# Who issues the four small copies ahead of each rotary multiply: SyncE or GpSimd

## The chip, the core and the metric

The kernel runs on one core of one Trainium2 chip. The metric is device microseconds of one execution; a measurement of this kernel can tell about 0.5% (6.4 us) from no change.

## What is computed

Two layers of a streaming encoder run on a prompt of 1024 tokens and a sample of 32 tokens with a past of 256, with shared weights. Layer 0 has a convolution branch and a forgetting attention. Layer 1 has a pooling branch and a sparse attention: a small indexer (4 heads of 64) scores all keys, each query keeps its best 256 (a threshold), and 8 heads of 64 attend under that mask. In layer 1 the queries, keys, index queries and index keys are rotated by their position:

```python
def rope(x, pos):
    ...
    x1, x2 = xf[..., : d // 2], xf[..., d // 2:]
    return jnp.concatenate([x1 * cos - x2 * sin, x2 * cos + x1 * sin], -1).astype(x.dtype)
```

## The kernel before, in words

Work is tiled with channels on the 128 partitions and up to 544 tokens along the row. A projection of 128 channels is 4 token groups of 24 matmuls (`proj_steps`, L207; operands are split in a high and a low part, so three products per block). While a projection runs on TensorE (PE), `tick` after every 8 matmuls runs deferred steps and background generators, so other stages are woven between.

A rotary call (`rope`, L982) works on a tile `rpx` [128, 544] that ScalarE (ACT) has filled from PSUM (L979, or L1209). Channel halves are 32 partitions apart, so `rope` first makes a copy `rps` with neighbouring blocks of 32 partitions exchanged: one DMA per block (L986), SBUF to SBUF, two for the 64 index-key channels and four for 128 channels. GpSimd (POOL) multiplies `rps` by the sine table (L987), VectorE (DVE) multiplies `rpx` by the cosine table in place (L988) and adds the two (L989). There is one buffer `rps`, so the copies of a call wait until the add of the call before has read it; L988 overwrites `rpx`, so it waits until the copies have landed.

There are 22 calls, 84 copies. In this text they are numbered in their order:

- ropes 0 and 1: index keys (64 channels, two copies each); ropes 2 to 5: index queries (two projections, each a 256-token and a 544-token half, four copies each). This is the index stage. Its results feed the index scores (L288, L289, then L1258 on ACT and L1260, L1262 on DVE), on which DVE's threshold search (L1088) and ACT's (L1112) stand.
- ropes 6 to 9: key and query of the first head pair (`qk1(0)`), while the masks are made (L1349 to L1391).
- ropes 10 to 21: key and query of the next three pairs, woven into the attention of the pair before (`attend`). After a key rope, `put_k` splits the result and `k_out` transposes it on PE (L295) for the output; after a query rope, `put_q` (L280 to L285) fills query tiles whose zero halves POOL writes (`blank_q`, L275 and L276).

All DMAs of the kernel before are issued by SyncE (SP), in one queue: weights (`wraw`, L114), value rows (`vf`, L448), gates (`sg`, L385), spills (L330, L331), outputs (`vo`, L1315; `ko`, L297) and the copies of L986. Every engine works through its own list in order; an instruction that waits holds up all behind it. The order of these lists is made by the scheduler of the tile framework from the program order, its priorities and its own cost model, so a change of who issues a DMA also moves other instructions.

Of the kernel before, what the change touches and what calls it, by code (L numbers as in the profile page):

```python
# [32 lines left out]
def tile_encoder(ctx: ExitStack, tc, A, O):  # L33
    nc = tc.nc
    pe, dve, act, pool, sp = nc.tensor, nc.vector, nc.scalar, nc.gpsimd, nc.sync
# [645 lines left out]
    with tc.tile_pool(name="p1", bufs=1, reuse_waits="tile") as p1:  # L681
# [82 lines left out]
        xs = p1.tile([128, 8, 128], FR, name="xs", tag="xrow", bufs=3)  # L764
# [217 lines left out]
    def rope(pl, x, t0, n, rows=128):  # L982
        xs = pl.tile([128, 544], FT, name="rps", tag="rps", bufs=1)
        for b in range(rows // 32):
            s = b ^ 1
            sp.dma_start(xs[32 * b:32 * b + 32, :n], x[32 * s:32 * s + 32, :n])  # L986
        pool.tensor_tensor(xs[:rows, :n], xs[:rows, :n], sinT[:rows, t0:t0 + n], op=OP.mult)  # L987
        dve.tensor_tensor(x[:rows, :n], x[:rows, :n], cosT[:rows, t0:t0 + n], op=OP.mult)  # L988
        dve.tensor_tensor(x[:rows, :n], x[:rows, :n], xs[:rows, :n], op=OP.add)  # L989
# [172 lines left out]
    with tc.tile_pool(name="p4", bufs=1, reuse_waits="tile") as p4:  # L1162
# [9 lines left out]
        def ev_ik(g, t0, n, ps):  # L1172
            act.activation(ikw[64:68, t0:t0 + n], ps[64:68], AF.Copy, scale=0.5)
            r = rope_in(p4, hold, "ik", g, ps[0:64], 1.0, 64)
            if g % 2 == 0:
                return
            t0, n = t0 - 256, n + 256
            rope(p4, r, t0, n, 64)
            cs = slice(t0, t0 + 512)
            act.activation(ikw[0:64, t0:t0 + n], r[0:64, :n], AF.Copy)  # L1180
            act.activation(kiA[0:64, cs], r[0:64, :512], AF.Copy)
            act.activation(kiB[64:128, cs], r[0:64, :512], AF.Copy)
            dve.tensor_tensor(kiA[64:128, cs], r[0:64, :512], kiA[0:64, cs].bitcast(FT), op=OP.subtract)
            dve.tensor_tensor(kiB[0:64, cs], r[0:64, :512], kiA[0:64, cs].bitcast(FT), op=OP.subtract)
# [16 lines left out]
        for p in range(2):  # L1201
            qA, qB = (p4.tile([128, SEQ - 256], FR, name=f"{nm}{p}") for nm in ("qiA", "qiB"))
            qz = blank_q(p4, f"qiz{p}", SEQ - 256)
            qi_st.append((qz, qA, qB))

            def ev_iq(g, t0, n, ps, p=p, qz=qz, qA=qA, qB=qB):
                if g == 1:
                    hold["iq"] = p4.tile([128, 544], FT, name="rpx", tag="rpx", bufs=2)
                    act.activation(hold["iq"][:, 256:512], ps, AF.Copy, scale=0.125)  # L1209
                    x, t0, n = hold["iq"][:, 256:512], 256, 256  # L1210
                else:
                    x = rope_in(p4, hold, "iq", g, ps, 0.125)
                    if g % 2 == 0:
                        return
                    t0, n = t0 - 256, n + 256
                rope(p4, x, t0, n)
                m = min(n, 512)
                cs = slice(t0 - 256, t0 - 256 + m)
                put_q(qz[:, :, cs], qA[:, cs], qB[:, cs], x[:, :m])
                if n > 512:  # L1220
                    dve.tensor_copy(iqS[:, p, :], x[:, 512:544])
            proj_cm(w1, 3072 + p * 128, 128, X1, ev_iq, range(1, 4))
# [265 lines left out]
    def qk1(p):  # L1488
# [6 lines left out]
        def ev_k(g, t0, n, ps):  # L1495
            r = rope_in(pq, hold, "k", g, ps, 1.0)
            if g % 2:
                rope(pq, r, t0 - 256, n + 256)
                put_k(kA, kB, t0 - 256, 512, r[:, :512])
                defer(6, k_out, 1, p, g // 2, n + 256, r, pq)  # L1500
                if n > 256:
                    dve.tensor_copy(qkS1[:, p, 1, :], r[:, 512:544])
# [106 lines left out]
```

## Time and profile before

| | us |
|---|---|
| median of 3 runs | 1274.49 |
| lowest and highest run | 1273.25, 1278.46 |
| the profiled execution's own time | 1278.22 |
| its span in the trace | 1276.2 |
| PE busy in the span | 1198.5 |
| DVE, ACT, POOL busy | 983.4, 712.5, 256.2 |
| granted TensorE clock, mean | 0.987 |

The profile page gives the busy time of each engine, the chain of work that ended last, and groups of instructions by line; the trace behind it can be asked for the instructions of a stretch in order of time, with the idle time before each and what ended it. Times in the trace are microseconds from the start of the span. Instructions that only issue a DMA are listed under their queue's engine (SPq for SP) and not counted as busy.

### The profile page before, as it was taken

To read this page: it belongs to the slowest core of one execution; us is meant where nothing else is said; L and a number is where in the kernel's file an instruction comes from. 1 tells how busy PE (TensorE), PEld (TensorE's weight loads), DVE (VectorE), ACT (ScalarE), POOL (GpSimd) and SP (SyncE) were. 2 spreads that over 40 slices of the span, in tenths; PEclk is the share of its full clock that TensorE was granted. 3 is DMA by queue.
4 is the path that set the end of the run, shared out by engine and by line. 5 is a ranking of instruction groups with operands and counts; after the bars stand their busy time and mean duration, and the time that the engine had idled before them with its cause. 6 is when DMAs were issued, how large, how long until landed. Compare 5 with 4: busy or idle time off the path is not lost.

```text
span 1276.2 us, 25219 instructions
## 1 busy us (share of the span) xinstructions
PE 1198.5 (94%) x9353; PEld 1136.2 (89%) x9353; DVE 983.4 (77%) x2053; ACT 712.5 (56%) x1533; POOL 256.2 (20%) x590
## 2 busy tenths in 40 slices
PE   8999999999998989999989979999898999879997
PEld 6999999988898977999988979999888888869997
DVE  5699999357877878558759958897678978886477
ACT  5111242378787876321366768888467778875110
POOL 0000033002433333000120336566211111100000
PEclk9999999999999999999999989999899999999999
DMA  7113422336322284642342232322323222633512
GB/s 223 51 34 97 122 54 63 94 100 187 85 84 84 67 260 131 192 131 101 112 106 62 69 84 68 84 64 64 85 68 97 71 72 80 199 117 123 161 38 99
DMA packets 163302, 130.29 MB, mean 102 GB/s; under 512 B 35850, under 2 KB 151010, under 8 KB 163180
## 3 DMA queue, kind: packets, MB, share of 16 engines
q1 hardware_dynamic: 163180, 128.69, 34.0%
q8 instruction: 73, 1.20, 0.4%
q14 instruction: 49, 0.40, 0.1%
HBM read 82.93 MB, written 40.31 MB: 97 GB/s over the span
## 4 chain that ended last, share of the span: by engine, by line
PE 59%; DVE 15%; ACT 14%; issue 5%; DMA 3%; SPq 1%; POOL 1%; DVEq 0%; ACTq 0%; POOLq 0%
PE bank L207 27%; PE bank L571 14%; PE bank L240 4%; PE bank L419 3%; ACT jka L1112 3%; PE bank L394 3%; DVE wt L1088 2%; ACT s L373 2%; PE bank L288 2%; ACT pth L107 2%; DVE ptl L108 1%; PE bank L289 1%; DVE s L370 1%; PE bank L223 1%; PE bank L252 1%
## 5 line engine op out<-in xcount | busy, mean ns | idle before, releaser
L870 DVE SCALAR_TENSOR_TENSOR acc<-apad,vT,acc 128x1086 f32<-128x1086 f32 x120 | 156.3, 1342 | 1.1
L108 DVE TENSOR_TENSOR ptl<-bank,pth 128x512 fp32r<-128x512 f32 (+1 forms) x160 | 99.1, 633 | 38.6 <-ACT pth L107 37.3
L207 PE MATMUL bank<-x1h,whi 128*128 128x256 f32 (+3 forms) x848 | 127.3, 289 | 0.1
L207 PE MATMUL bank<-x1h,wlo 128*128 128x256 f32 (+3 forms) x848 | 127.3, 291 | 0.0
L207 PE MATMUL bank<-x1l,whi 128*128 128x256 f32 (+3 forms) x848 | 126.3, 289 | 0.0
L207 PEld LDWEIGHTS bank<-x1h,wlo 128*128 128x128 f32 (+1 forms) x848 | 115.8, 193 | 1.6
L207 PEld LDWEIGHTS bank<-x1h,whi 128*128 128x128 f32 (+1 forms) x848 | 113.5, 189 | 1.9 <-ACT rpx L979 0.3
L207 PE MATMUL bank<-x0h,whi 128*128 128x256 f32 (+1 forms) x768 | 113.4, 288 | 1.5 <-ACT kr L810 1.0
L207 PEld LDWEIGHTS bank<-x1l,whi 128*128 128x128 f32 (+1 forms) x848 | 113.7, 190 | 0.9
L373 ACT ACTIVATE s<-s,mn 128x896 f32<-128x896 f32 (+7 forms) x128 | 98.8, 773 | 24.7 <-DVE mn L370 23.6
L419 PE MATMUL bank<-ident,s 128*128 128x128 f32 x576 | 96.2, 279 | 17.4 <-DVE ptl L108 10.8
L207 PE MATMUL bank<-x0h,wlo 128*128 128x256 f32 (+1 forms) x768 | 111.7, 286 | 0.0
L207 PE MATMUL bank<-x0l,whi 128*128 128x256 f32 (+1 forms) x768 | 110.4, 284 | 0.0
L108 DVE TENSOR_TENSOR wlo<-wraw,whi 128x1024 fp32r<-128x1024 f32 (+2 forms) x62 | 75.3, 1215 | 43.2 <-ACT whi L107 43.2
L107 ACT ACTIVATE pth<-bank 128x512 fp32r<-128x512 f32 (+1 forms) x160 | 85.8, 549 | 34.3 <-PE bank L419 32.3
L207 PEld LDWEIGHTS bank<-x0h,whi 128*128 128x128 f32 x768 | 101.2, 189 | 3.7 <-ACT kr L810 1.3
L207 PEld LDWEIGHTS bank<-x0h,wlo 128*128 128x128 f32 x768 | 100.8, 189 | 0.8
L207 PEld LDWEIGHTS bank<-x0l,whi 128*128 128x128 f32 x768 | 100.0, 188 | 0.7
L1112 ACT ACTIVATE jka<-sc,neg 128x768 bf16<-128x768 f32 (+2 forms) x96 | 99.3, 1035 | 2.0
L107 ACT ACTIVATE whi<-wraw 128x1024 fp32r<-128x1024 f32 (+2 forms) x62 | 65.0, 1050 | 55.7 <-PE bank L207 36.0
L394 PE MATMUL bank<-pth,v 128*128 128x256 f32 x320 | 92.0, 306 | 3.6 <-ACT pth L107 3.2
L419 PEld LDWEIGHTS bank<-ident,s 128*128 128x128 f32 x576 | 66.2, 140 | 32.6 <-DVE ptl L108 12.2
(422 smaller groups left out, 2695.0 us busy)
## 6 DMA issues: line engine op xcount, KB each, us to landing
wraw<-in_o_w_in_dram SPq DMA_DIRECT2D x26, 512.0 KB, 4.0
wraw<-in_e_w_in_dram SPq DMA_DIRECT2D x24, 512.0 KB, 4.1
sgd<-sgc SPq DMA_DIRECT2D x32, 128.0 KB, 3.0
out_dram<-ko SPq DMA_DIRECT2D x16, 256.0 KB, 2.3
vf<-vd SPq DMA_DIRECT2D x16, 256.0 KB, 3.1
ckb<-ckd SPq DMA_DIRECT2D x8, 512.0 KB, 4.7
sg<-sgd SPq DMA_DIRECT2D x32, 128.0 KB, 2.7
wraw<-in_e_w_out_dram SPq DMA_DIRECT2D x8, 512.0 KB, 4.2
```

Source lines behind the costliest of these rows:

```text
L107: up = act.activation(hi, src, AF.Copy)
L108: eng.tensor_tensor(lo, src, hi.bitcast(FT), op=OP.subtract)
L207: pe.matmul(ps, w[:, k, :], x[g][:, k, :], start=i == 0, stop=i == 23)
L240: pe.matmul(ps, x[g][:, k, off:off + rows], ws[k // 4][wi][:, k % 4, :], start=i == 0, stop=i == 23)
L288: pe.matmul(ps, qz[:, e, c0:c0 + m], k2[:, k0:k0 + n], start=True, stop=False)
L373: act.activation(s[:, :n], s[:, :n], AF.Exp, bias=mn[:, c:c + 1], scale=-1.0, accum_out=grp[p, i][0][:, j, e:e + 1])
L394: pe.matmul(po[:, j0 * 128:j0 * 128 + w], v2[e][:, k, :], src[:, b0:b0 + w], start=k == 0 and x == 0, stop=k == 2 * i + 1 and x == 1)
L419: pe.transpose(ps[:, c:c + 128], pt[j][:, k * 128:(k + 1) * 128], ident)
L571: pe.matmul(ps, lhs(j, k), ws[k // 4][wi][:, k % 4, :], start=i == 0, stop=i == 23)
L870: dve.scalar_tensor_tensor(ac, apad[c][:, j:j + 1086], vT[:, c, j:j + 1], ac, op0=OP.mult, op1=OP.add)
L1088: ins = dve.tensor_scalar(jkd[:, :n], x if b > 15 else x.bitcast(U16), (cand[:, c:c + 1].bitcast(FT) if b > 15 else cl[:, c:c + 1]), None, ...
L1112: act.activation(jka[:, :n], sct[COL[ND + j]], AF.Sign, bias=neg[:, j:j + 1].bitcast(FT), accum_out=cnta[:, j:j + 1]))
```

## The change

The copies of the rotary halves are issued by POOL instead of SP. Nothing else is edited:

```diff
         xs = pl.tile([128, 544], FT, name="rps", tag="rps", bufs=1)
         for b in range(rows // 32):
             s = b ^ 1
-            sp.dma_start(xs[32 * b:32 * b + 32, :n], x[32 * s:32 * s + 32, :n])
+            pool.dma_start(xs[32 * b:32 * b + 32, :n], x[32 * s:32 * s + 32, :n])
         pool.tensor_tensor(xs[:rows, :n], xs[:rows, :n], sinT[:rows, t0:t0 + n], op=OP.mult)
```

The scheduler then orders the lists of all engines anew, from the index stage to the end of the attention of layer 1. On POOL, in the index stage (ropes 1 to 4; `rps` is the exchanged copy, `sinT` the sine table):

```order
 L987 TENSOR_TENSOR rps<-rps,sinT 64x512
+L986 DMA rps<-rpx 32x544 x2
 L987 TENSOR_TENSOR rps<-rps,sinT 64x544
+L986 DMA rps<-rpx 32x256 x4
 L987 TENSOR_TENSOR rps<-rps,sinT 128x256
-L987 TENSOR_TENSOR rps<-rps,sinT 128x544
+L986 DMA rps<-rpx 32x544 x4
+L987 TENSOR_TENSOR rps<-rps,sinT 128x544
```

The copies of each rope stand right ahead of its multiply, behind the multiply of the rope before.

On DVE, at the start of the index stage (rope 0; `wlo` is the low part of a weight block, `pwl` that of the pooling weights):

```order
+L988 TENSOR_TENSOR rpx<-rpx,cosT 64x512
 L1017 COPY thr<-ci 128x7
+L989 TENSOR_TENSOR rpx<-rpx,rps 64x512
 L108 TENSOR_TENSOR wlo<-wraw,whi 128x1024
 L1042 COPY cand<-ci 128x4
-L988 TENSOR_TENSOR rpx<-rpx,cosT 64x512
-L989 TENSOR_TENSOR rpx<-rpx,rps 64x512
-L108 TENSOR_TENSOR pwl<-pwr,pwh 128x512
 L1183 TENSOR_TENSOR kiA<-rpx,kiA 64x512
 L1184 TENSOR_TENSOR kiB<-rpx,kiA 64x512
+L108 TENSOR_TENSOR pwl<-pwr,pwh 128x512
```

Both steps of rope 0 now stand ahead of the `wlo` pass that stood ahead of them. The same holds for rope 3, further down the same list (`sc` is the score of the first query tile):

```order
-L108 TENSOR_TENSOR wlo<-wraw,whi 128x1024
 L988 TENSOR_TENSOR rpx<-rpx,cosT 128x544
-L1260 TENSOR_SCALAR sc_8051<-rl,iwt 128x384
 L989 TENSOR_TENSOR rpx<-rpx,rps 128x544
-L1262 SCALAR_TENSOR_TENSOR sc_8051<-rl,iwt,sc_8051 128x384
-L1221 COPY iqS<-rpx 128x32
+L108 TENSOR_TENSOR wlo<-wraw,whi 128x1024
```

Here too `wlo` moved from ahead of the rope's two steps to behind them.

On SP, where the attention of layer 1 begins (ropes 7 to 11; `vf` is the value rows of a head):

```order
+L297 DMA out_dram<-ko 128x4x128 x2
 L303 DMA out_dram<-rpx 32x128
-L986 DMA rps<-rpx 32x512 x2
-L986 DMA rps<-rpx 32x544 x4
-L114 DMA wraw<-in_o_w_in_dram 128x8x128
-L986 DMA rps<-rpx 32x512 x2
+L114 DMA wraw<-in_o_w_in_dram 128x8x128
 L448 DMA vf<-vd_166 128x8x64
-L986 DMA rps<-rpx 32x512 x2
 L385 DMA sg<-sgd_159 128x256
```

The first `vf` load stood between the second and the third copy of rope 10; now it follows the weight load directly.

## Rows read from the trace of the kernel before

**Rows 1.** The page, busy time, share of the span and instructions by engine
```profile
PE 1198.5 (94%) x9353; PEld 1136.2 (89%) x9353; DVE 983.4 (77%) x2053; ACT 712.5 (56%) x1533; POOL 256.2 (20%) x590
```

**Rows 2.** The chain that ended last, in order of time: start, us, what
```profile
663.72 1.88 DMA rps<-rpx
```

**Rows 3.** Busy time by stretch: us, busy of each engine, PEclk, DMA share, GB/s
```profile
634.00:674.00 40.00, 36.61 (x270) 34.92 (x269) 20.27 (x34) 23.93 (x56) 8.08 (x7) 0.96 0.41 112
674.00:738.00 64.00, 58.93 (x431) 54.97 (x430) 59.70 (x162) 41.82 (x93) 10.98 (x47) 0.99 0.24 65
738.00:742.00 4.00, 0.00 (x0) 0.00 (x0) 0.00 (x0) 0.67 (x3) 0.00 (x0) 0.50 0.88 244
...
742.00:905.00 163.00, 158.45 (x1274) 157.42 (x1275) 131.57 (x352) 127.91 (x262) 96.51 (x278) 0.97 0.25 70
...
955.00:965.00 10.00, 6.91 (x45) 6.51 (x44) 8.43 (x13) 6.38 (x13) 2.68 (x2) 0.83 0.37 88
```

**Rows 4.** In order of time, four engines: start, us, instruction, [idle before, releaser]
```profile
734.94 1.22 DVE L108 TENSOR_TENSOR wlo<-wraw,whi 128x1024 fp32r<-128x1024 f32 x1
...
736.18 0.39 SPq L114 DMA_DIRECT2D wraw<-in_o_w_in_dram  x1
...
741.33 0.38 ACT L1312 ACTIVATE vo<-bank 128x256 f32<-128x256 f32 x1 [8.98 <-DMA vd<-vo]
...
742.07 0.69 PE L1308 MATMUL bank<-ident,vr 128*128 128x128 f32 x2 [7.54 <-ACT vr L1302]
```

**Rows 5.** PE in order of time, the two waits for a rotary add
```profile
915.86 1.12 PE L295 MATMUL bank<-ident,rpx 128*128 128x128 f32 x4 [3.54 <-DVE rpx L989]
...
959.44 1.11 PE L295 MATMUL bank<-ident,rpx 128*128 128x128 f32 x4 [3.09 <-DVE rpx L989]
```

**Rows 6.** The instructions of the tile rps: durations in ns min/median/max, first and last start
```profile
L986 SPq DMA_DIRECT2D rps<-rpx x84: 507/584/1438, 635.0 to 1117.4; - x84
L987 POOL TENSOR_TENSOR rps<-rps,sinT x22: 974/1374/1902, 638.1 to 1119.6; 128x544 f32<-128x544 f32 x10, 128x512 f32<-128x512 f32 x8, 128x256 f32<-128x256 f32 x2, 64x512 f32<-64x512 f32 x1
```

**Rows 7.** SP in order of time: the copies of ropes 0, 3 and 6, and around rope 10
```profile
634.99 1.24 SPq L986 DMA_DIRECT2D rps<-rpx  x2
...
653.59 2.41 SPq L986 DMA_DIRECT2D rps<-rpx  x4
...
908.64 9.01 SPq L986 DMA_DIRECT2D rps<-rpx  x7
...
944.90 0.39 SPq L114 DMA_DIRECT2D wraw<-in_o_w_in_dram  x1
947.91 1.14 SPq L986 DMA_DIRECT2D rps<-rpx  x2
949.10 0.58 SPq L448 DMA_DIRECT2D vf<-vd  x1
949.72 1.25 SPq L986 DMA_DIRECT2D rps<-rpx  x2
```

**Rows 8.** POOL in order of time: the multiplies of ropes 0, 3, 6 and 10
```profile
638.13 1.28 POOL L987 TENSOR_TENSOR rps<-rps,sinT 64x512 f32<-64x512 f32 x1 [10.50 <-DMA rps<-rpx]
...
657.57 1.36 POOL L987 TENSOR_TENSOR rps<-rps,sinT 128x544 f32<-128x544 f32 x1 [4.51 <-DMA rps<-rpx]
...
913.31 1.77 POOL L987 TENSOR_TENSOR rps<-rps,sinT 128x512 f32<-128x512 f32 x1 [10.78 <-DMA rps<-rpx]
...
955.68 1.28 POOL L987 TENSOR_TENSOR rps<-rps,sinT 128x512 f32<-128x512 f32 x1 [4.60 <-DMA rps<-rpx]
```

**Rows 9.** DVE in order of time: around ropes 0 and 3, and rope 2's add
```profile
639.61 1.23 DVE L108 TENSOR_TENSOR wlo<-wraw,whi 128x1024 fp32r<-128x1024 f32 x1 [1.81 <-ACT whi L107]
...
641.61 0.68 DVE L989 TENSOR_TENSOR rpx<-rpx,rps 64x512 f32<-64x512 f32 x1
...
653.10 0.43 DVE L989 TENSOR_TENSOR rpx<-rpx,rps 128x256 f32<-128x256 f32 x1 [0.63 <-POOL rps L987]
...
659.04 1.23 DVE L108 TENSOR_TENSOR wlo<-wraw,whi 128x1024 fp32r<-128x1024 f32 x1 [4.17 <-ACT whi L107]
...
661.15 0.72 DVE L989 TENSOR_TENSOR rpx<-rpx,rps 128x544 f32<-128x544 f32 x1
```

## Prediction

> **What bounds the kernel now.** I read the page first: PE is busy in 94% of the span, POOL in 20% [rows 1]. So the change can only cost or give time where PE stands still for a rope, or where a rope sets the start of something that PE later stands still for. Then I read the chain of waits, to see whether the copies are in it at all. They are: there are pieces in the index stage, one of them at 663.72 [rows 2].
>
> The stretches say what follows from that [rows 3]. From 674 to 738 DVE is busy 59.70 of 64 us: as soon as index scores exist it is full, with scores and threshold search. From 738 to 742 PE does nothing. From 742 to 905 PE is busy 158.45 of 163 us, so what is late at 742 is late at the end. Why PE stands at 742 is read step by step [rows 4]: DVE comes to a `wlo` pass only at 734.94, deep in its list behind the search; SP's weight load waits for it until 736.18, the stores of `vo` queue behind that load; ACT waits 8.98 us for those stores, and PE 7.54 us for ACT. DVE's list is the clock of this stage, and it starts when the index ropes are done. A shift of the index ropes should therefore reach the end one for one.
>
> Later, PE waits for a rotary add twice: 3.54 us at 915.86 (rope 6) and 3.09 us at 959.44 (rope 10) [rows 5]. Ropes 11 to 21 have no such wait, nor have 7 to 9: other work covers them. That cover is some microseconds deep, since a rope is started well ahead of the attention that uses it; if it is gone, each of them costs what it is late.
>
> **What one rope costs.** SP needs 584 ns (median) for an issue [rows 6], four in a row take 2.41 us, two 1.24 us [rows 7]. Rope 3: issues from 653.59 to 656.00, multiply at 657.57 [rows 7, 8], so 1.57 us from the end of the issues to the multiply. The rest (multiply, add) stays as it is. With an issue on POOL of g us, a rope of four copies changes by 4g - 2.41, one of two by 2g - 1.24, if the 1.57 us stay.
>
> No row shows a DMA issued by POOL. Bounds for g: from below SP's price, 0.60 us (2.41 / 4); below that I do not go, since POOL's own instruction with the least work on `rps` takes 0.974 us. From above POOL's slowest multiply, 1.902 us [rows 6]. I take the middle of POOL's shortest and its median multiply, (0.974 + 1.374) / 2 = 1.17 us, since the new issue is an instruction of POOL, next in its list to just these. Then four copies take 4.68 us instead of 2.41.
>
> **The change part by part.**
>
> SP loses 84 issues, 84 x 0.584 = 49 us of queue time. It issued the first copy of rope 3 at 653.59, 0.06 us after rope 2's add had ended (653.10 + 0.43 = 653.53) [rows 7, 9], so there POOL can gain no earlier start; and SP's other DMAs are not what ends PE's waits, with the one exception below. Value: nothing, hidden behind PE.
>
> POOL gains 84 issues, 84 x 1.17 = 98 us; it goes from 256 to 354 us of 1276, some 28%. Behind an issue that waits for ACT's eviction or for the add of the rope before stand that rope's own multiply, which would wait too, and some memsets of `qz` and `sc`, whose readers come later. I cost these at nothing; their cover is that POOL is idle most of the time.
>
> Index stage. Ropes 0 to 4 run strictly one after another, because `rps` has one buffer: each starts when the one before is added. Two have two copies, three have four: 2 x (2g - 1.24) + 3 x (4g - 2.41) = 16g - 9.71, at 1.17 us +9.0 us. Against that, DVE's list has changed. Rope 0's multiply ends at 638.13 + 1.28 = 639.41, but its add starts at 641.61, because `wlo` (639.61, 1.23 us) and L988 came between [rows 8, 9]: 2.2 us. Rope 3's multiply ends at 658.93, its add starts at 661.15, again behind `wlo`: 2.2 us. In the new list both steps stand ahead of `wlo`, so some 2.1 us each come back, 4.2 in all. What is late instead is `wlo`, which is for a projection later than the one then running, so I put nothing on it. Sum: 16g - 13.9 = **+4.8 us**, passed on at 742.
>
> Rope 6. From its first issue at 908.64 to its multiply at 913.31 are 4.67 us [rows 7, 8]; with POOL 4g + 1.57 = 6.25. PE already waits for it [rows 5], so this is 4g - 3.1 = **+1.6 us**.
>
> Rope 10. Its third and fourth copy are issued behind the first `vf` load, at 949.72, done at 950.97; its multiply starts at 955.68, 4.7 us later instead of 1.57 [rows 7, 8]. In the new lists `vf` is right behind the weight load of 944.90, some 3.7 us earlier, and out of the way. With POOL the multiply could start at 947.91 + 6.25 = 954.2, 1.5 us earlier, and DVE, which splits `vf` ahead of this rope, has it earlier as well. At best the wait of 3.09 us goes, and with it what the clock loses after it: granted 0.83 in the ten microseconds around it [rows 3], 1.7 us. So between 0 and -4.8; I take the middle, **-2.4 us**. When this stall goes, late next is DVE's work at the start of attention.
>
> Sum: 20g - 19.4 = 4.8 + 1.6 - 2.4 = **+4.0 us**. The profiled execution took 1278.22 us (span 1276.2), 3.7 us above the median of 1274.49; on the median the forecast is 1278.5 us, a change of 0.3%.
>
> The Trainium skill, DMA: Bandwidth & Descriptors, section Latency and other measured facts, says that the first byte of a DMA issued by GpSimd comes after about 1 us, of one issued by SP after about 0.6 us. No row here shows the former. As an estimate from that page, 0.4 us more on each of the six ropes counted would make the sum +6.4 us, on the edge of slower. The same page, section Issuing engines are not separate DMA queues, says that DMAs of all issuers share the same 16 engines and that spreading them saves only issue time. By it rope 10's copies gain nothing from another queue, only from `vf` being issued earlier; the sum without that term would be +6.4 us.
>
> **The rivals.** By the formula the change is nothing at g = 0.97, faster by over 0.5% (6.4 us) below 0.65, slower by as much above 1.29.
>
> - Faster: POOL issues at SP's price, 0.60 us, and rope 10's wait goes wholly: 12 - 17.0 - 4.8 = -9.8 us, 1264.7. For it: the credit of 4.2 us on DVE and the 3.1 us of rope 10 stand in rows. Against it: no POOL instruction on this tile takes under 0.97 us.
> - Slower: a POOL issue is held up beside DVE as its multiply is. That ranges from 0.97 to 1.90 us for near sizes; rope 6's 128x512 took 1.77 where rope 10's took 1.28 [rows 6, 8]. Place: the index ropes, where DVE has other work beside POOL's. At g = 1.6, +12.6 us, 1287.1; it decides above 1.29 us. For it: the measured spread; against it: DVE is busy only half of that stage, 20.27 of 40 us [rows 3].
> - Later landing: POOL's copies arrive later after their issue than SP's. From the end of the issues to the multiply are 1.57 us at rope 3, but 638.13 - 636.23 = 1.90 at rope 0 [rows 7, 8]. With 0.4 us more on six ropes the sum is 4.0 + 2.4 = +6.4 us, 1280.9. Against it: a copy moves the same bytes whoever issues it.
> - Nothing: the exchange is hidden anyway, because PE has other matmuls at 634 to 674 (busy 36.61 of 40) and the scheduler moves them up: 1274.5 us. Against it: DVE's list, not PE's, is full afterwards.
>
> **How the numbers follow.** Forecast case (g from 0.65 to 1.29): 0.43. Slower: 0.29; it gets much, since the upper bound of g lies farther off than the lower and no row excludes it. Faster: 0.15. Later landing: 0.08, on the edge, so half of it counts as slower. Nothing: 0.05. The 6.4 us are about what a measurement of this kernel can tell from no change. Same: 0.43 + 0.04 + 0.05 = 0.52; slower: 0.29 + 0.04 = 0.33. The range reaches from the faster rival, 1265, to the slower one with rope 10's wait left as it is, 1274.5 + 15.0, 1290.
>
> **What would show it.** In the changed profile: the issues of L986 on POOL, and the time from the first of four to the multiply, 6.2 us expected against 4.0; the time from rope 0's first copy to rope 4's add, the last before the scores, some 5 us longer; PE's wait at 742 some 5 us longer or later; the wait for rope 6 at 5 us; the wait for rope 10 short or gone. The prediction is wrong if the wait at 742 has gone (then the index stage is not passed on), if ropes 11 to 21 appear among PE's waits, or if PE's new list, rather than a rope, opens or closes gaps of this size.

## The result, and the profile after

| | before | after |
|---|---|---|
| median, us (11 runs each) | 1276.75 | 1284.52 |
| lowest and highest, us | 1270.65, 1283.58 | 1280.76, 1290.74 |
| profiled execution, its own time, us | 1278.22 | 1281.78 |

The ratio is 1.0062, 95% interval 1.0043 to 1.0081: slower by 0.62%, 7.8 us by the medians. The forecast was +4.0 us; the time lies in the range, and by the medians the case "slower by over 0.5%" came (0.33), though the interval reaches below 0.5%. The two profiled executions differ by less than the medians (3.6 us): after's lies below its median, before's above. So the main readings are compared below with further traces.

The page after, busy time, and its queues (packets, MB, share of 16 engines):

```profile
PE 1200.7 (94%) x9353; PEld 1140.4 (89%) x9353; DVE 985.2 (77%) x2053; ACT 710.1 (55%) x1533; POOL 299.9 (23%) x674
...
q1 hardware_dynamic: 159148, 123.27, 32.3%
q0 software_dynamic: 2688, 5.42, 1.8%
```

Against [rows 1] POOL alone has grown by more than some 2 us: 44 us for 84 issues, not 98. The 2688 packets of the copies are in a queue of their own now. The tile `rps` says the price of one (ns min/median/max):

```profile
L986 POOL DMA_DIRECT2D rps<-rpx x84: 496/496/696, 635.7 to 1117.4; - x84
L987 POOL TENSOR_TENSOR rps<-rps,sinT x22: 977/1366/1898, 640.5 to 1121.6; 128x544 f32<-128x544 f32 x10, 128x512 f32<-128x512 f32 x8, 128x256 f32<-128x256 f32 x2, 64x512 f32<-64x512 f32 x1
```

g is 0.50 us, less than SP's 0.584 [rows 6] and far from the 1.17 taken, and no issue took more than 0.70. In the median the multiply is as long as it was. And yet the ropes are not shorter. POOL in order of time, ropes 0 to 4 and 7:

```profile
635.73 1.21 POOL L986 DMA_DIRECT2D rps<-rpx  x2 [8.88 <-ACT rpx L979]
...
640.46 1.29 POOL L987 TENSOR_TENSOR rps<-rps,sinT 64x512 f32<-64x512 f32 x1 [1.92 <-DMA rps<-rpx]
643.65 1.03 POOL L986 DMA_DIRECT2D rps<-rpx  x2 [1.90 <-DVE rpx L989]
647.97 1.89 POOL L987 TENSOR_TENSOR rps<-rps,sinT 64x544 f32<-64x544 f32 x1 [3.29 <-DMA rps<-rpx]
651.16 2.00 POOL L986 DMA_DIRECT2D rps<-rpx  x4 [1.31 <-DVE rpx L989]
654.55 1.54 POOL L987 TENSOR_TENSOR rps<-rps,sinT 128x256 f32<-128x256 f32 x1 [1.39 <-DMA rps<-rpx]
657.47 2.00 POOL L986 DMA_DIRECT2D rps<-rpx  x4 [1.38 <-ACT qiz L280]
661.17 1.90 POOL L987 TENSOR_TENSOR rps<-rps,sinT 128x544 f32<-128x544 f32 x1 [1.70 <-DMA rps<-rpx]
664.39 2.01 POOL L986 DMA_DIRECT2D rps<-rpx  x4 [1.32 <-DVE rpx L989]
669.25 0.98 POOL L987 TENSOR_TENSOR rps<-rps,sinT 128x256 f32<-128x256 f32 x1 [2.86 <-DMA rps<-rpx]
...
918.05 2.01 POOL L986 DMA_DIRECT2D rps<-rpx  x4 [1.38 <-DVE nd L1348]
924.72 1.89 POOL L987 TENSOR_TENSOR rps<-rps,sinT 128x544 f32<-128x544 f32 x1 [4.66 <-DMA rps<-rpx]
```

Two things are to be seen. First, the issues start late: rope 0's add ends at 643.08 (642.40 + 0.68) and rope 1's first issue comes at 643.65, 0.57 us later, where SP took 0.06. Second, from the end of the issues to the multiply pass 3.5 us (640.46 - 636.94), 3.3, 1.4, 1.7, then 2.9 for rope 4 and 4.66 for rope 7. By SP it was 1.4 to 2.0 in the same ropes. Not every rope is late, so it is not a price of POOL's issue. SP's own loads, in order of time, tell which of these are:

```profile
633.70 1.10 SPq L1192 DMA_DIRECT2D pwr<-in_o_pool_w_dram  x1
...
635.55 0.90 SPq L1245 DMA_DIRECT2D icd<-in_cache_dsa_idx_k_dram  x2
...
644.25 0.37 SPq L114 DMA_DIRECT2D wraw<-in_o_w_in_dram  x1
...
655.53 0.37 SPq L114 DMA_DIRECT2D wraw<-in_o_w_in_dram  x1
...
665.85 0.37 SPq L114 DMA_DIRECT2D wraw<-in_o_w_in_dram  x1
...
918.88 0.38 SPq L114 DMA_DIRECT2D wraw<-in_o_w_in_dram  x1
```

Ropes 0, 1, 4 and 7, the late ones, have a load issued right before or among their copies: the pooling weights and caches at 633.70 to 636.45, the weight blocks at 644.25, 665.85 and 918.88 (512 KB each). Ropes 2 and 3 have none that close. In before, SP's single list put the copies first: rope 7's last copy was issued at 918.31, the weight load behind it at 918.92, and the pooling weights behind rope 0. And it is the new DVE list that makes them meet: `wlo` (643.01, 1.21 us, moved in the first DVE piece of the change) now stands right behind rope 0's add; it frees `wraw`, so SP's load leaves at 644.25, while rope 1's copies, which waited for the same add, are issued. On DVE in the profile after:

```profile
642.40 0.68 DVE L989 TENSOR_TENSOR rpx<-rpx,rps 64x512 f32<-64x512 f32 x1
643.01 1.21 DVE L108 TENSOR_TENSOR wlo<-wraw,whi 128x1024 fp32r<-128x1024 f32 x1
```

Copy by copy the order shows within one rope. Of rope 7's four copies two are issued ahead of the load (918.05 and 918.59) and land 1.9 and 2.0 us after the start of their issue, two behind it (919.08 and 919.57) and land after 4.6 and 5.0. In between, from 920.5 to 922.0, the load's queue moves packets and that of the copies none; the whole list of queues with packets in these 1.5 us is

```profile
q1 hardware_dynamic: 549, 0.28, 79.2%
```

A load that left earlier costs less: in before one leaves 1.45 us ahead of rope 1's first copy (640.87 against 642.32), and the multiply follows their last issue after 2.0 us. Ropes 6, 8 and 10 of after are late as well, 2.5 to 2.65 us, without a weight load among their copies; what these meet was not tested.

What PE makes of it, in order of time:

```profile
654.57 2.07 PE L207 MATMUL bank<-x1h,whi 128*128 128x256 f32 x8 [3.73 <-ACT rpx L979]
...
745.31 0.69 PE L1308 MATMUL bank<-ident,vr 128*128 128x128 f32 x2 [7.70 <-ACT vr L1302]
...
917.54 1.12 PE L295 MATMUL bank<-ident,rpx 128*128 128x128 f32 x4 [3.51 <-DVE rpx L989]
...
940.37 0.74 PE L207 MATMUL bank<-x1h,whi 128*128 128x256 f32 x4 [1.69 <-ACT rpx L979]
...
951.78 1.21 PE L207 MATMUL bank<-x1h,whi 128*128 128x256 f32 x8 [2.65 <-ACT rpx L979]
...
968.94 0.63 PE L295 MATMUL bank<-ident,rpx 128*128 128x128 f32 x4 [1.62 <-DVE rpx L989]
```

The wait at 742 [rows 4] is as long and 3.24 us later, of which 0.83 us were there before rope 0 (its eviction ended at 635.43 instead of 634.60). Rope 6 [rows 5] is unchanged: 3.51 us. Rope 10's wait is gone, and three new ones stand in its place: 1.69 and 2.65 us for ACT's evictions into `rpx`, and 1.62 us for rope 11's add.

The two waits for ACT come from ACT's list, which is ordered anew too and is not among the lists shown with the change. The second eviction of rope 9 (L979, 128x288) stood ahead of the eight reads of rope 8 (the first is L280); now it stands behind them, and ACT waits 1.92 us for rope 8's add before it starts to read. In before:

```profile
933.83 0.41 ACT L979 ACTIVATE rpx<-bank 128x288 f32<-128x288 f32 x1 [0.90 <-PE bank L207]
934.62 0.40 ACT L280 ACTIVATE qz<-rpx 64x256 fp32r<-64x256 f32 x1
```

and in after:

```profile
935.27 0.42 ACT L280 ACTIVATE qz<-rpx 64x256 fp32r<-64x256 f32 x1 [1.92 <-DVE rpx L989]
...
939.92 0.39 ACT L979 ACTIVATE rpx<-bank 128x288 f32<-128x288 f32 x1
```

PE waits for this eviction at 940.37. Rope 9's copies are issued behind it, at 940.61 instead of 934.60; so rope 9's add ends 37.7 us after rope 6's first issue instead of 34.6, ACT reads rope 9 later, and the next eviction, at 951.37 behind these reads, makes PE wait the second time. Rope 7's late landing is not in this chain: its add ends 17.1 us after rope 6's first issue, in before 16.8, and rope 8's add 25.0 us after it, in before 25.9.

### The profile page after: what moved, and what is told of

The parts are those of the page before. It is cut to its first block, busy times and chain, and to the rows that moved or that the text cites. A ratio compares the mean times of both kernels' runs of the same rounds, so it can differ in the third digit from the quotient of the medians.

```text
span 1279.7 us, 25222 instructions
## 1 busy us (share of the span) xinstructions
PE 1200.7 (94%) x9353; PEld 1140.4 (89%) x9353; DVE 985.2 (77%) x2053; ACT 710.1 (55%) x1533; POOL 299.9 (23%) x674
## 3 DMA queue, kind: packets, MB, share of 16 engines
q0 software_dynamic: 2688, 5.42, 1.8%
## 4 chain that ended last, share of the span: by engine, by line
PE 60%; DVE 15%; ACT 12%; issue 6%; DMA 4%; POOL 2%; SPq 0%; DVEq 0%; ACTq 0%; POOLq 0%
PE bank L207 26%; PE bank L571 14%; PE bank L240 4%; PE bank L419 3%; PE bank L394 3%; DVE wt L1088 2%; DMA rps<-rpx 2%; ACT jka L1112 2%; ACT s L373 2%; PE bank L288 2%; DVE s L370 2%; PE bank L289 2%; DVE ptl L108 1%; ACT pth L107 1%; PE bank L223 1%
## 5 line engine op out<-in xcount | busy, mean ns | idle before, releaser
L919 POOL TENSOR_SCALAR s<-ckb,ncq 128x896 f32<-128x896 f32 (+3 forms) x64 | 53.2, 842 | 183.9 <-DMA ckb<-ckd 105.0
```

The source lines that it names most:

```text
L919: pool.tensor_scalar(s[:, :n], ckb[:, :n], ncq[:, qi, h:h + 1], 1.0, op0=OP.add, op1=OP.mult)
```

## The experiments

The question is whether the loss is the issuer, the meeting with SP's loads, the new lists, or the clock. A useful ruler is the time from the end of rope 0's eviction to PE's restart after the wait at 742: 107.47 us in the first trace of before, 110 in that of after. It leaves out what differed earlier, but not the clock in between.

| label | copies issued by POOL | ruler, us | ratio to before, 95% interval |
|---|---|---|---|
| before, three traces | none | 107.5, 107.6, 107.4 | 1 |
| after, two traces | all | 109.9, 110.1 | 1.0062 (1.0043 to 1.0081) |
| e1_index_pool | ropes 0 to 5 | 109.2 | 1.0043 (1.0025 to 1.0061) |
| e2_late_pool | ropes 6 to 21 | 107.6 | 1.0027 (1.0009 to 1.0045) |
| e3_act_queue | none (all by ACT) | 108.2 | 1.0105 (1.0071 to 1.0139) |
| e4_half_half | half of ropes 2 to 21 | 104.0 | 1.0047 (1.0028 to 1.0066) |
| e8_two_rps_pool | all, two `rps` early | 109.4 | 1.0043 (1.0019 to 1.0067) |
| e9_half_index | half of ropes 2 to 5 | 103.9 | 0.9999 (0.9981 to 1.0017) |
| e10_ropes_2_to_5_pool | ropes 2 to 5 | 108.9 | 1.0024 (1.0006 to 1.0041) |
| e11_before_plus_9 | none | 106.0 | 1.0019 (1.0000 to 1.0038) |
| e12_late_pool_not7 | 6 and 8 to 21 | 107.3 | 0.9995 (0.9976 to 1.0014) |

**Where the loss is.** In both kernels `rope` gets its issuer from the call:

```diff
-            sp.dma_start(xs[32 * b:32 * b + 32, :n], x[32 * s:32 * s + 32, :n])
+            eng.dma_start(xs[32 * b:32 * b + 32, :n], x[32 * s:32 * s + 32, :n])
```

> Copies of ropes 0 to 5 (index stage) on POOL, those of ropes 6 to 21 on SP. Theory 'late ropes': the cost sits in the index stage, where five ropes run one after another and a POOL-issued rope starts about 0.5 us later after the add of the rope before and lands later; rope 4's add ends near 670 instead of 667, PE's wait at 742 comes about 3 us later, and most of the loss of the changed kernel is here: +3 to +8 us against the kernel before. Rival 'later ropes': the loss comes from ropes 6 to 21 and the new lists of the attention: then this kernel is within 2 us of the kernel before. Rival 'given back': the wait at 742 is later, but PE makes it up by 816, as the two traces suggest; then also within 2 us.

> Copies of ropes 0 to 5 on SP, those of ropes 6 to 21 on POOL. Theory 'late ropes' (index stage): rope 4's add ends within 1.5 us of 667.2, PE waits at 742 as before, and the kernel is within 2 us of the kernel before, since PE waited for none of ropes 11 to 21 in the changed kernel's trace. Rival 'later ropes': +4 to +8 us here, with PE's waits for ACT evictions at 940 and 952 (1.7 and 2.7 us in the changed kernel) again.

Measured +0.43% and +0.27%, some 5.5 and 3.4 us: both halves lose, and together they make the 0.62% within their intervals. Neither theory had that: "late ropes" expected nothing from ropes 6 to 21, "later ropes" nothing from the index stage. But e1 does not lose all of it in the index stage: its ruler is 1.7 us longer. Its 12 runs have a mean granted clock of 0.9802, the 29 of before beside them 0.9852; at 0.69 us for 0.001 (see the point on the clock in the next section) this is an estimated 3.5 us more. That the ropes make the clock fall is not shown. PE's waits at 940, 951 and 969 are in e2 again (1.70, 2.64 and 1.60 us), with ACT's order of after.

**Whose path is slow.** All copies by ACT, and half of each rope by each:

```diff
-            sp.dma_start(xs[32 * b:32 * b + 32, :n], x[32 * s:32 * s + 32, :n])
+            act.dma_start(xs[32 * b:32 * b + 32, :n], x[32 * s:32 * s + 32, :n])
```

```diff
-            sp.dma_start(xs[32 * b:32 * b + 32, :n], x[32 * s:32 * s + 32, :n])
+            (sp if b < 2 else pool).dma_start(xs[32 * b:32 * b + 32, :n], x[32 * s:32 * s + 32, :n])
```

> All 84 copies issued by ACT: off SP as in the changed kernel, but not by POOL. Theory 'the issuer's path is slow' : what is late comes from POOL (start 0.5 us after the add, 2.5 to 3.1 us from the last issue to the multiply at ropes 4 to 6); from ACT the start is within 0.1 us and the multiply follows the last issue after 1.5 to 1.9 us, as from SP. Rival 'collision': the copies lose because they no longer stand in one queue with SP's loads, which run ahead and share the DMA engines with them; then from ACT too 2.5 to 3.1 us. Time of the whole: ACT pays about 84 x 0.6 = 50 us of issue, and an issue that waits for the add of the rope before holds up ACT's evictions, so 0 to +15 us; only the ropes' times decide between the two.

> Of each rope the first two copies are issued by SP, the third and fourth by POOL, at the same time and of the same size. Theory 'the issuer's path is slow': POOL's land later than SP's in the same rope by 0.5 us or more from the end of their issue. Rival 'collision with SP's loads': both land alike. Issue time of four copies drops from 2.4 to 1.2 us, so if landing were equal, ropes 2 to 5 would be 1.2 us shorter each and the kernel up to 4 us faster than before; by 'the issuer's path is slow' the gain is eaten: within 2 us of the kernel before.

By ACT the start is nearer to SP's (0.2 to 0.3 us after an add), but the multiply follows the last issue after 3.7 us at rope 0, 1.7, 1.5, 3.5 at rope 3, 2.2 at rope 4. SP's loads left at 634.24 to 636.5 (rope 0's copies: 634.51), at 643.11 (rope 1's: 642.15 to 643.30), at 654.81 (rope 3's: 653.61 to 656.05) and at 662.61 (rope 4's from 663.49). So an issuer that is not POOL is late in the same way, where a load leaves just before or among its copies; rope 1's last copy, whose issue began 0.42 us ahead of the load, is in time: "the issuer's path is slow" falls, "collision" stands. In the half-and-half kernel the landing is alike for both issuers (DMA issues: KB each, median us from issue to landing):

```profile
rps<-rpx SPq DMA_DIRECT2D x22, 68.0 KB, 2.1
rps<-rpx POOLq DMA_DIRECT2D x20, 68.0 KB, 2.1
rps<-rpx SPq DMA_DIRECT2D x18, 64.0 KB, 2.5
...
rps<-rpx POOLq DMA_DIRECT2D x16, 64.0 KB, 2.1
```

Its index stage is 3.5 us shorter than before's, as hoped, and the whole is 0.47% slower: it loses everything, and more, behind rope 6. That loss I did not take apart; PE has a wait of 2.18 us for an eviction into `rpx` at 934.93, with ACT's order of after. By ACT the whole is slowest: 84 issues of 0.6 us stand in a list that PE waits for (10.07 us at 742 instead of 7.5). Its ruler is only 0.7 us longer, so where the rest of its 13 us is lost is not shown.

**Once more without a change.** The kernel before twice, the changed one once:

> The kernel before, unchanged, for a second trace. In the traces of the changed kernel and of the three kernels with copies from POOL so far, 2.9 us are lost at about 1200 to 1220, where the clock is granted 0.83 and the code is the same; the first trace of before has no such drop. Theory 'late ropes' (the loss is waits that ropes make): the drop at 1200 is chance and will stand in this trace or not, whoever issues the copies. Rival 'clock': before never has it (1.00 at 1200 to 1220 and at 1100 to 1140), and a good part of the loss is clock that the changed kernel loses after the ropes.

> The kernel before, unchanged, for a third trace: as for the second. By 'clock' again no drop at 1100 to 1140 and none at 1200 to 1220; by chance a drop in at least one of the two traces is likely, since four of four kernels with copies from POOL have it.

> The changed kernel, unchanged, for a second trace. By 'clock' drops at 1100 to 1140 and at 1200 to 1220 again, some 2 and 2.9 us; by chance not both. By 'late ropes' the wait at 742 again 2.4 to 3.3 us later than in before, counted from rope 0's eviction.

Two readings of mine rested on one execution. The wait of 3.09 us for rope 10 [rows 5] is in the second trace of before

```profile
954.01 0.66 PE L295 MATMUL bank<-ident,rpx 128*128 128x128 f32 x4 [0.72 <-DVE rpx L989]
```

and in the third

```profile
956.89 0.74 PE L295 MATMUL bank<-ident,rpx 128*128 128x128 f32 x4 [1.87 <-DVE rpx L989]
```

The ruler and the waits at 940 and 951, on the other hand, repeat within 0.2 us, and the same ropes are late (rope 4 by 2.9 and 3.4 us from the last issue). The clock has two levels, 1.00 and 0.50 in the rows (2.4 and 1.2 GHz); a mean between them says that part of a stretch ran at the lower. In the stretch 1183 to 1209, behind the last rope, it is 1.00 in the first and third trace of before, 0.93 in the second, 0.89 and 0.88 in the two of after. So "before never has it" is wrong; yet all nine traces with copies from POOL lie below 1.00 there (0.87 to 0.95), and of the five without, two. In the first trace of after (columns as in [rows 3]):

```profile
1183.00:1209.00 26.00, 25.96 (x213) 23.98 (x212) 10.94 (x31) 5.64 (x14) 0.00 (x0) 0.89 0.57 174
```

**Is it the single buffer?** Two `rps` in the index stage, all copies by POOL (`bufs` is passed by the calls of the index stage):

```diff
-        xs = pl.tile([128, 544], FT, name="rps", tag="rps", bufs=1)
+        xs = pl.tile([128, 544], FT, name="rps", tag="rps", bufs=bufs)
```

> Copies on POOL as in the changed kernel, but with two buffers rps in the index stage, so that a rope's copies need not wait for the add of the rope before. Theory 'late ropes': the start of 0.5 us after the add and the late landing lie beside the rope before; rope 4's add ends at 667 or sooner, the wait at 742 is not later than in before, and the kernel is 3 to 6 us faster than the changed one (within 4 us of before). Rival 'clock', or 'later ropes': the index stage gains, but the time stays within 3 us of the changed kernel.

Rope 4's add ends 29.2 us after rope 0's first issue (35.1 in after, 32.2 in before), and still PE restarts at 109.4 by the ruler. PE waits 1.85 us at 652.97 for ACT's eviction (L979). Rope 3 has a weight load among its copies (653.93; the copies from 653.50) and is multiplied 3.9 us after the last issue. Rope 5 then waits for `rpx`, which has two buffers: ACT fills it at 665.34 and 667.36, after it has read rope 3, and the copies start at 668.04. "Late ropes" was right on the chain and wrong on what follows from it; the gain of 0.2% against the changed kernel is inside the intervals.

**Which ropes, and does halving pay?** Ropes 0 and 1 back on SP; ropes 2 to 5 halved or wholly on POOL; the rest on SP:

> Ropes 0 and 1 and the first two copies of ropes 2 to 5 by SP, the third and fourth copy of ropes 2 to 5 by POOL; ropes 6 to 21 by SP. Where all 22 ropes were halved, PE stood 3.4 us earlier at 742 than in the first trace of before (counted from 645), and lost some 7 us between 903 and 1153. If a shorter index stage is passed on ('the index stage counts'), this kernel keeps the 3 to 4 us: 1271 to 1274 against 1276. Rival 'given back': the wait is made up before 973, within 2 us of before. Rival 'clock': PE reaches 1200 earlier than in before and may or may not lose 1.5 to 2.9 us there.

> Only ropes 2 to 5 (index queries) on POOL; ropes 0 and 1 and 6 to 21 by SP. Theory 'collision': what is slow from POOL is rope 0 and 1, because SP's pooling-weight and cache loads stand ahead of their copies instead of behind, and the weight load comes at rope 1; with these two on SP again they take 1.5 to 2.1 us from the last issue to the multiply, and ropes 2 to 4 on POOL are no longer than by SP: rope 4's add at most 667, the wait at 742 not later than in before. Rival 'the issuer's path is slow': each of ropes 2 to 5 is 0.5 to 1 us longer than by SP, the wait at 742 is 1.5 to 3 us later.

In e10 SP issues weight loads at 650.38 and 663.70; POOL in order of time:

```profile
649.67 2.19 POOL L986 DMA_DIRECT2D rps<-rpx  x4 [1.37 <-ACT whi L107]
655.11 0.98 POOL L987 TENSOR_TENSOR rps<-rps,sinT 128x256 f32<-128x256 f32 x1 [3.24 <-DMA rps<-rpx]
657.11 2.00 POOL L986 DMA_DIRECT2D rps<-rpx  x4 [1.03 <-ACT qiz L280]
660.69 1.90 POOL L987 TENSOR_TENSOR rps<-rps,sinT 128x544 f32<-128x544 f32 x1 [1.58 <-DMA rps<-rpx]
664.86 2.00 POOL L986 DMA_DIRECT2D rps<-rpx  x4 [2.27 <-DVE iqS L1221]
668.47 0.98 POOL L987 TENSOR_TENSOR rps<-rps,sinT 128x256 f32<-128x256 f32 x1 [1.60 <-DMA rps<-rpx]
```

Rope 2 has a load among its copies and is late, 3.24 us; rope 3 has none, rope 4 has one that left 1.16 us ahead of its first copy, and they need 1.58 and 1.60, about as by SP. In e9 the same load leaves at 650.51, right behind rope 2's last POOL issue (its issue begins at 650.34):

```profile
649.62 1.22 POOL L986 DMA_DIRECT2D rps<-rpx  x2 [1.37 <-ACT whi L107]
652.45 0.97 POOL L987 TENSOR_TENSOR rps<-rps,sinT 128x256 f32<-128x256 f32 x1 [1.61 <-DMA rps<-rpx]
```

and rope 2 waits 1.61. So in this pair order decides: a copy issued ahead of the load passes, one issued behind it waits. How far ahead is enough, other ropes tell: e9's last copy was begun 0.17 us ahead and lands 1.98 us later; rope 1's last copy in after was begun 0.07 us ahead (644.18 against 644.25) and lands 3.65 us later. Ropes 0 and 1, on SP again, wait 1.7 to 2.1 us. But ropes 2 to 4 are not free on POOL, as "collision" had it: each starts 0.55 to 0.62 us after the add, and e10's ruler is 1.4 us longer than before's. Halving makes each shorter by SP's early start and half the issue time; its ruler is 3.6 us shorter. The time of the whole does not show it: 0.9999. Its trace has the clock at 0.87 in 1183 to 1209 and at 0.92 in 1107 to 1153; the mean clock of its 12 runs is 0.9827, of 87 runs of before 0.9841. By the 0.69 us for 0.001 that is about 1 us of where the gain went; the rest is open.

**The clock by itself.**

```diff
-        next(sample)
+        next(sample), [pe.matmul(ps_pj()[:, :256], cat[0][TT[4][0]][:, k % 8, TT[4][1]:TT[4][1] + 128], W[0][0][0][:, 0, :], start=True, stop=True) for k in range(9 * l)]
```

(`l` is the layer, 0 or 1.)

> The kernel before, all copies by SP, with 9 matmuls of 128x256 more (0.28 us each, 2.5 us, results unused) on PE ahead of the output layer, behind the last rope. Lists of the other engines have the same instructions. Theory 'clock' (where PE stands in time decides whether the clock drops at 1200): this kernel has the drop to 0.83 at 1200 to 1220 too, though no copy is issued by POOL, and costs 2.5 + 2.9 = 5.4 us at most, ratio 1.004. Rival 'the drop comes with POOL's copies': no drop, at most 2.5 us, ratio 1.002 or less.

Busy time and clock at 1200 to 1220:

```profile
1200.00:1220.00 20.00, 20.00 (x154) 18.90 (x153) 7.24 (x17) 3.30 (x8) 0.00 (x0) 0.83 0.24 75
```

The drop is there with every copy on SP, so it needs no copies by POOL. But the price of 5.4 us is not: 1.0019 is about what the nine matmuls cost alone (2.5 us), and this trace was the slowest of the kernel's runs. A later PE does not have to lose clock. Its ruler of 106.0, with before's lists up to there, belongs to the clock too: this trace lacks before's drop to 0.91 at 660 to 680. So 1.5 us is how far one such drop moves the ruler. The other rulers are not corrected for it: after has no drop there but one at 0.50 from 655.4 to 660.4, behind PE's wait of 3.73 us, and e4 and e9 have 1.00 at 660 to 680, so part of their shorter rulers may be clock.

**One rope back.** As e2, but rope 7 on SP (`NR` counts the calls; the eighth is rope 7):

```diff
-        xs = pl.tile([128, 544], FT, name="rps", tag="rps", bufs=1)
+        xs = pl.tile([128, 544], FT, name="rps", tag="rps", bufs=1); NR.append(0); eng = pool if len(NR) > 6 and len(NR) != 8 else sp
```

> As the kernel with ropes 6 to 21 on POOL, but rope 7 back on SP, where its copies stand ahead of the next weight load (wraw) again. In the traces with ropes 6 to 21 on POOL that load starts beside rope 7's copies, they land 4.3 to 4.5 us after the last issue, and PE waits 1.7 and 2.6 us at about 940 and 951 for ACT's evictions into rpx, whose buffers ropes 7 and 8 still hold. Theory 'collision': rope 7's multiply follows its last issue after about 1.9 us again, both waits go, and most of the 0.27% of that kernel with them: ratio 0.999 to 1.001. Rival 'many small losses': the two waits go, but the 3 us are spread over ropes 10 to 21 and stay: ratio 1.002 to 1.003. Rival 'new lists': other waits of PE of the same sum open between 903 and 973.

SP issues rope 7's copies at 916.81 and 919.28 and the weight load at 919.94, and POOL multiplies after 1.83 us instead of 4.66:

```profile
914.17 1.77 POOL L987 TENSOR_TENSOR rps<-rps,sinT 128x512 f32<-128x512 f32 x1 [2.14 <-DMA rps<-rpx]
921.67 1.36 POOL L987 TENSOR_TENSOR rps<-rps,sinT 128x544 f32<-128x544 f32 x1 [5.73 <-DMA rps<-rpx]
```

Both waits of PE are gone, the one for rope 11 is there (2.24 us at 966.88; e2 has 1.60 at 968.11), and the time is before's: 0.9995 against 1.0027. The numbers are those that "collision" forecast, but the cause is another. ACT's list has before's order again in e12:

```profile
934.70 0.41 ACT L979 ACTIVATE rpx<-bank 128x288 f32<-128x288 f32 x1 [0.40 <-PE bank L207]
...
935.52 0.42 ACT L280 ACTIVATE qz<-rpx 64x256 fp32r<-64x256 f32 x1
```

and rope 7, though its copies land sooner, is not done sooner: its add ends 17.7 us after rope 6's first issue, in e2 16.9. The other traces agree. In the eight with this eviction ahead of the reads of rope 8 (before three times, e1, e9, e10, e11, e12) rope 9's add ends 33.7 to 34.9 us after rope 6's first issue; in the five with it behind them (after twice, e2, e4, e8) 36.7 to 37.7, and PE waits for the eviction. (e3 has a third order.) So the waits of e2 come with the new order of ACT's list; that rope 7's landing costs anything there is not shown.

Nor is all of the 0.32% between e2 and e12 these waits. The mean clock of e12's runs is 0.9858, of the 17 of before beside them 0.9830, which at 0.69 us for 0.001 is an estimated 2 us in e12's favour (in e2 0.9844 against 0.9852). At equal clock e2 would be some 3 us slower than before and e12 some 1.5.

## Why the prediction was right and wrong

Slower: the sign of the forecast held, and the place of its largest term (index stage, passed on at 742), but that place holds 2.5 of the 7.8 us. Two of the things that the prediction named as signs of its being wrong came: rope 11 is among PE's waits, and a new list, ACT's, opens gaps. The sum lay in the range by errors that cancel and by terms that it did not have:

- **The price g.** Taken 1.17, bounded below at 0.60; measured 0.50, under the bound. The nearest row was SP's issue, not POOL's multiply. By the formula g = 0.50 alone would have given -9.4 us, the rival "faster".
- **The start.** "There POOL can gain no earlier start" put SP and POOL level. POOL starts 0.57 us after a DVE add, 0.30 after an ACT eviction, SP 0.06 after an add: four ropes of the chain, +2.1 us. No term had this.
- **The 1.57 us to the multiply.** "If the 1.57 us stay" was the weak step: 3.5, 3.3, 1.4, 1.7 and 2.9 us at ropes 0 to 4, against 1.9, 2.0, 1.5, 1.6 and 1.4 by SP: +4.3 us. The rival "later landing" was on this spot with 0.4 us on each of six ropes; it is 1.3 to 2.8 on the few that meet a load. "SP's other DMAs ... Value: nothing" belongs here: SP's list, freed of the copies, lets its loads leave beside them.
- **The credit of 4.2 us on DVE.** It came: rope 0's add now follows its multiply after 0.65 us and rope 3's after 0.03 instead of 2.2 each, 3.7 us. But "what is late instead is `wlo` ... so I put nothing on it" is the step that let the load in: a moved `wlo` moves the weight load that waits for it. At ropes 2 and 4 the add is 0.45 us later behind its multiply, so 3.3 us in all.
- **The multiply.** "The rest (multiply, add) stays as it is" missed 1.1 us: ropes 2 and 3 take 1.54 and 1.90 us instead of 0.98 and 1.36. Rope 3's ran with DVE idle in before and beside L988 in after.
- **The index stage**: +4.8 forecast, rope 4's add measured +2.9 from rope 0's first issue, which is the sum of starts +2.1, issues -1.4, landing +4.3, multiplies +1.1 and multiply to add -3.3; +2.5 by the ruler. Passed on nearly one for one, as said: DVE comes to the `wlo` pass of [rows 4] 67.8 us after rope 4's add in before and 67.2 in after. (In e8 it is 72.8, so rope 4 is not what it waits for there.)
- **Rope 6**: +1.6 forecast, nothing measured: 4.66 us from first issue to multiply (4.67 before), because four issues take 2.0 us and the landing 2.6, where the four of before took 3.1 and the landing 1.6.
- **Rope 10**: -2.4 forecast. The wait was 3.09, 0.72 and 1.87 us in three traces of one kernel; I read one. It went; three waits of 1.7, 2.65 and 1.6 us opened. The step that failed here is "other work covers them": the cover of ropes 7 to 10 was an order of ACT's list, which the change moved, and no term looked at ACT's list; what uncovers rope 11 stays open.
- **The clock**: no term. The mean granted clock of 12 runs of after is 0.9816; of the 87 runs of before that the comparisons hold 0.9841. Among these 87 runs 0.001 goes with 0.69 us (correlation -0.87), so some 1.7 of the 7.8 us go with the clock. Why it falls more often is not settled.

As an estimate the parts make up the whole: 2.5 us at 742, 6.0 us of new waits behind rope 6 less 1.9 (the mean of rope 10's three), and 1.7 us of clock are 8.3 against 7.8 measured.

The Trainium skill, DMA: Bandwidth & Descriptors, section Latency and other measured facts, has a first byte after 1 us for GpSimd and 0.6 for SP. No run here shows such a gap: where no other packet moves, the first packet of a copy starts 1.10 us after the start of its issue by POOL (median of 13 in after), 1.17 by SP (8 in before) and 1.18 by ACT (10 in e3), and the medians to landing over all copies with a recorded landing are 2.05, 2.02 and 2.05. The Trainium skill's section Issuing engines are not separate DMA queues, on the same page, fits what decided here: another issuer does not keep a copy out of a load's way. By it I would have struck rope 10's term (+6.4 us); that is nearer to 7.8, but by luck, since rope 10's wait did go.

## What to carry to other kernels

A DMA taken out of a shared queue loses its place ahead of that queue's loads: before moving it, list which large load will leave beside it, and which instruction releases that load. A list that gives a rope's steps back to DVE earlier moves what they displaced; follow that too, up to the DMA that waits for it. Compare the lists of all engines, also of one that the change does not touch: here an eviction that moved behind eight reads on ACT made the waits that a late copy seemed to make. And when an experiment gives the forecast number, look whether the wait went for the forecast reason. And read a wait that carries a term in more than one trace: here one was 3.09, 0.72 and 1.87 us without any change.

## What was not expected of the hardware

- A DMA issue costs POOL 0.50 us, SP 0.58, ACT 0.60 (medians): the issuer that looked dearest is the cheapest.
- POOL begins it 0.57 us after the DVE instruction that it waited for, against 0.06 by SP and 0.2 to 0.3 by ACT.
- The same stretch of the output layer, with no copy near it, is granted 1.00 in one trace and 0.87 to 0.95 in others of the same or nearly the same program; the runs of before spread over 14 us, and most of that goes with the clock.
